# First stage of a two-block transformer kernel: loads interleaved and moved to another queue, the S5 scan split in two halves, top-k searches spaced

## The chip, the cores and the metric

The kernel runs on one core of a Trainium2 chip. The metric is the device time in microseconds (us) of one launch. TensorE is written PE (its weight loads PEld), VectorE DVE, ScalarE ACT, GpSimd POOL, and SyncE SP; SP does nothing here but issue DMAs.

## The reference

Two layers work on `x` of 256 tokens by 2048 features, all in float32.

```python
# block 1
z = rmsnorm(x) @ w_in                 # 2048 x 5128: q, k, v, o, gates, u
hm = mlstm(silu(conv(q,k)), v, gates) # 4 heads of 256, two chunks of 128 tokens
ys = s5_groups(u, ...)                # 64 groups of 16 channels, 64 complex states each:
                                      #   s[t] = a*s[t-1] + B u[t];  y = C s + D u;  GLU
h = x + concat(hm, ys) @ w_out
q = rmsnorm(h) @ wq                   # peer: 8 heads, two halves of 128 keys each
s1, i1 = top_k(q1 @ keys1, 16); s2, i2 = top_k(q2 @ keys2, 16)
idx, gate = top_k over the 256 sums, 16 of them, softmax
h = h + sum_e gate_e * gelu(h . u_tab[idx_e]) * v_tab[idx_e]   # 16384 experts
# block 2: three kinds of attention, gates, and a SwiGLU with 5632 hidden features
```

## The kernel before, in words

**Matrix products.** `gemm` (L245) goes over column tiles of at most 512. For each it loads the weights in chunks of 128 x 1024 (512 KB, two steps of k) by `raw` (L228) into four rotating buffers from SP's queue, splits each half chunk into a rounded part `wh` on ACT (L241) and a rest `wl` on DVE (L242), and runs three matmuls for each of two token blocks (L268 to L270): 12 matmuls of 128 x 512 a chunk. After each chunk it calls `step`, and after each tile a callback that evicts the accumulators.

**Side work.** Everything else is written as generators in three lists (`add_side`). `step` (L169) advances the first generator of each list to its next `yield`, so the number of yields sets behind how many chunks a piece of side work stands in the program. `drain` runs what is left. The queues of the engines are not in program order: `TileContext(nc, schedule_with_timeline_sim=True)` lays them out by simulated times, and takes later work first where its inputs and buffers are ready.

**First stage** (`phase_a`, L744). `x` is loaded in eight pieces, transposed by PE, and evicted to `xh` and `xl` (`put_T`, L306), with the sums of squares on ACT. Then come three tiles of `w_in` that give u and the gates, and eight that give v, q, k, o for two halves of the heads, with two steps a chunk (64 chunks). S5 runs as side work in list 0: `s5_params`, `s5_taps` for each quarter q of the groups, `s5_put_u` (u goes to DRAM and comes back reordered in eight DMAs of 128 KB, in runs of 128 bytes), `s5_in` for each quarter, which writes `Vt`, `s5_states`, a chain of 31 steps of four GpSimd operations over all groups, then for each quarter `s5_out` and `s5_glu`. `s5_out` loads a 1 MB table `t0` back from DRAM, and `s5_glu` moves its result through DRAM in eight DMAs and one load. All these DMAs are SP's. The mixing product `w_out` starts with the S5 half, so it needs `ys`.

**Expert selection** (`peer`). `peer_scores` (L915) runs four tiles of `wq` with one step a chunk. Each tile adds two `tops` generators, each with four searches (L928 to L932). `peer_choose` has 33 yields for each of two token blocks, and its products with one-hots are L986 (DVE), L988 (POOL) and L991 (DVE). `peer_gates` makes the 256 x 16384 gate matrix, two tokens at a time: one-hots on DVE (L1051, L1052), their products with the gates on POOL (L1053, L1054), a matmul (L1060), a copy on ACT (L1063), and sums and products into `AT` on DVE (L1070, L1071, L1073). It yields once, then twice in every fourth of 128 iterations and once in the others: 161 yields. `peer_u` (L1015) runs 32 tiles of 8 chunks with one step a chunk, evicts (L1023, then L1030 or L1034 into `AT`), and calls `drain`. A gate iteration that stands in the program behind the callbacks of n tiles multiplies into what these n tiles have written of `AT`. `peer_v` reads, for each of its products, all 256 tokens of `AT`.

Of the kernel before, what the change touches and what calls it, by code (L numbers as in the profile page):

```python
# [23 lines left out]
D = 2048  # L24
# [95 lines left out]

def later(f):
    yield from f()
# [28 lines left out]
class Kern:  # L151
    def __init__(self, tc, A, ctx):
        self.tc, self.nc, self.A, self.ctx = tc, tc.nc, A, ctx
        self.side = [[], [], []]
        self.GB, self.heads = {}, set()
        self.raw_slots, self.raw_n = [None], 0
# [87 lines left out]

    def gemm(self, wname, widths, KT, xh, xl, cb, steps=1, base=0, ks=None):  # L245

        nc, w = self.nc, self.A[wname]
        off = base
        ka, kb = ks or (0, KT)
        sc = self.stp[1]  # L250
        for i, wn in enumerate(widths):
            P = [self.psG.tile([128, 512], F32, name="g") for _ in range(2)]
            per = RC // wn
            sub = max(1, sc // wn)
            for k0 in range(ka, kb, per):
                kn = min(per, kb - k0)
                r = self.raw(bass.AP(tensor=w.tensor, offset=w.offset + off + 128 * k0 * wn,
                                     ap=[[kn * wn, 128], [1, kn * wn]]), kn * wn)
# [12 lines left out]
                self.step(steps)  # L271
            cb(i, P)
            off += 128 * KT * wn
        return off

    def rstd(self, pool, ss, n, name="rstd", bufs=2):
# [3 lines left out]
        return self.rsqrt(pool, v, name, bufs)  # L280

    def rsqrt(self, pool, v, name, bufs):

        V = self.nc.vector
        w = list(v.shape)
        r = pool.tile(w, F32, name=name, bufs=bufs)
# [30 lines left out]
    def norm_r(self, work, ss, name="rstd"):  # L317
# [3 lines left out]
        return self.rstd(work, st, D, name)  # L321
# [27 lines left out]
    def s5_params(self, p):  # L349
        nc = self.nc  # L350
        prm = p.tile([128, 96 + 2048], F32, name="s5prm")
        nc.sync.dma_start(prm, self.A["s5p"])
# [62 lines left out]
        for r in range(2):  # L415
# [22 lines left out]
        self.Vt = self.xx.tile([128, 32, 2, 32], F32, name="X1")  # L438
        yield

    def s5_taps(self, p, q):
# [38 lines left out]
        nc.sync.dma_start(dr.rearrange("p g o -> p (g o)"), self.A["s5d"][:, q * 256:(q + 1) * 256])  # L480
# [3 lines left out]
        nc.sync.dma_start(bass.AP(tensor=k.tensor, offset=k.offset + q * 16 * 3840 + 7 * 256,  # L484
# [3 lines left out]
    def s5_put_u(self, p, uT):  # L488
# [13 lines left out]
    def s5_in(self, p, q):  # L502
# [21 lines left out]
        for a in range(2):  # L524
            m = 8 * q + 4 * a
            V.tensor_copy(self.Vt[:, :, :, m:m + 4].rearrange("p c r g -> p r g c"), bv[:, a])
        yield

    def s5_states(self, p):

        E, Vt = self.nc.gpsimd, self.Vt
        S = self.S = p.tile([128, 32, 2, 32], F32, name="s5b")
        a8r, a8i = self.a8
        E.memset(S[:, 0], 0.0)
        for c in range(31):
            t1 = p.tile([128, 2, 32], F32, name="s5t1", bufs=2)
            t2 = p.tile([128, 2, 32], F32, name="s5t2", bufs=2)
# [7 lines left out]
    def s5_out(self, p, q, yg):  # L545

        nc, V, q5 = self.nc, self.nc.vector, self.s5
        pw, pn, cn, U, S = q5["pw"], q5["pn"], q5["cn"], self.U[q], self.S
        ms = slice(8 * q, 8 * q + 8)
        t0 = p.tile([128, 8, 16, 16], F32, name="s5t0")  # L550
        k = self.Kd
        nc.sync.dma_start(t0.rearrange("p i g o -> p (i g o)"),
                            bass.AP(tensor=k.tensor, offset=k.offset + q * 16 * 3840,
                                    ap=[[256, 8], [3840, 16], [1, 2048]]))
# [13 lines left out]
        for hf in range(2):  # L568
# [7 lines left out]
            for a in range(2):  # L576
                for r in range(2):
                    for gr in range(4):
                        m = a * 4 + gr
                        nc.tensor.matmul(b[gr * 32:gr * 32 + 32, a * 128:(a + 1) * 128], S[pr, :, r, 8 * q + m],  # L580
# [6 lines left out]
        nc.scalar.activation(yg[:, 16 * q:16 * q + 16].rearrange("p g c -> p (g c)"), b, AF.Gelu)  # L587
        yield

    def s5_glu(self, p, q, yg, ys):  # L590

        nc, V = self.nc, self.nc.vector
# [23 lines left out]
    def s5_all(self, p, uT, ys):  # L616
        yield from self.s5_put_u(p, uT)
        self.glu = p.tile([128, 8, 2, 128], F32, name="s5c")
        self.nc.sync.dma_start(self.glu.rearrange("p a b c -> p (a b c)"), self.A["glu"])
# [5 lines left out]
        yg = self.xx.tile([128, 64, 32], F32, name="X1")  # L625
# [118 lines left out]
    def phase_a(self):  # L744
        nc, V, A = self.nc, self.nc.vector, self.A
        with ExitStack() as ex:
            xh = self.act.tile([128, KD, T], F32R, name="xh")
            xl = self.act.tile([128, KD, T], F32R, name="xl")
            with self.tc.tile_pool(name="pa0", bufs=1) as p0:
                nc.gpsimd.dma_start(self.vecs, A["vecs"])  # L750
                ss = p0.tile([128, 2, 4], F32, name="lss")
                X = [p0.tile([128, D], F32, name=f"X{tb}") for tb in range(2)]
                for q in range(4):
                    s = slice(q * 512, (q + 1) * 512)
                    for tb in range(2):
                        nc.sync.dma_start(X[tb][:, s], A["x"][tb * 128:(tb + 1) * 128, s])
                    self.put_T(X, xh, xl, self.vecs[:, 0:16], q)
                    for tb in range(2):
                        self.sumsq(p0, ss[:, tb, q:q + 1], X[tb][:, s])
                r = self.norm_r(self.c, ss, "rA")  # L760
# [6 lines left out]
            nc.sync.dma_start(bg, A["b_gates"])  # L767
# [70 lines left out]
            for tb in range(2):  # L838
                nc.sync.dma_start(X[tb], A["x"][tb * 128:(tb + 1) * 128, :])
# [75 lines left out]
    def peer_scores(self, p, w, xh, xl, r):  # L915
# [8 lines left out]
        def tops(i, tb, sc):  # L924
            for n in range(4):
# [7 lines left out]
                yield  # L933
# [808 lines left out]
```

## Time and profile before

| | us |
|---|---|
| three runs: median (lowest to highest) | 3687.51 (3687.36 to 3690.19) |
| the profiled execution | 3691.2 |
| its span, first to last instruction | 3689.4 |
| PE busy, share of the span | 3576.1, 97% |
| DVE, ACT, POOL busy | 2710.1, 2007.8, 572.4 |

All stretches below are counted from the span's first instruction. A matmul's recorded end is modelled, so a busy PE means that matmuls follow one another without a gap, and the granted clock (1.00 is the full level) says how fast they run.

### The profile page before, as it was taken

To read this page: it belongs to the slowest core of one execution; us is meant where nothing else is said; L and a number is where in the kernel's file an instruction comes from. 1 tells how busy PE (TensorE), PEld (TensorE's weight loads), DVE (VectorE), ACT (ScalarE), POOL (GpSimd) and SP (SyncE) were. 2 spreads that over 40 slices of the span, in tenths; PEclk is the share of its full clock that TensorE was granted. 3 is DMA by queue.
4 is the path that set the end of the run, shared out by engine and by line. 5 is a ranking of instruction groups with operands and counts; after the bars stand their busy time and mean duration, and the time that the engine had idled before them with its cause. 6 is when DMAs were issued, how large, how long until landed. Compare 5 with 4: busy or idle time off the path is not lost. (4 is left out here: it accounts for less than half of the span.)

```text
span 3689.4 us, 52827 instructions
## 1 busy us (share of the span) xinstructions
PE 3576.1 (97%) x17438; PEld 2959.4 (80%) x17438; DVE 2710.1 (73%) x5604; ACT 2007.8 (54%) x3492; POOL 572.4 (16%) x670
## 2 busy tenths in 40 slices
PE   9897999999999999999999899999999999999999
PEld 7676887788887778888888777887888888888889
DVE  8685779779999857777777878877666666666554
ACT  5555655555555555555555565765445555555443
POOL 1060002225555400001000121001111000000000
PEclk9998999999999999999999999999999999999999
DMA  7656555555555567778777564677776577777665
GB/s 206 184 160 154 185 177 160 169 174 179 172 167 164 169 223 257 255 255 296 257 256 238 197 219 156 190 246 267 257 252 219 171 224 229 232 226 218 186 198 162
DMA packets 228514, 766.07 MB, mean 208 GB/s; under 512 B 40528, under 2 KB 44496, under 8 KB 226192
## 3 DMA queue, kind: packets, MB, share of 16 engines
q1 hardware_dynamic: 197728, 647.89, 55.6%
q0 software_dynamic: 30512, 114.81, 10.2%
q8 instruction: 137, 2.24, 0.2%
q14 instruction: 137, 1.12, 0.1%
HBM read 753.23 MB, written 9.37 MB: 207 GB/s over the span
## 5 line engine op out<-in xcount | busy, mean ns | idle before, releaser
L241 ACT ACTIVATE wh<-raw 128x512 fp32r<-128x512 f32 (+1 forms) x2064 | 1287.5, 628 | 1299.0 <-PE g L269 657.3
L242 DVE TENSOR_TENSOR wl<-raw,wh 128x512 fp32r<-128x512 f32 (+1 forms) x2064 | 1447.1, 715 | 621.7 <-ACT wh L241 534.9
L268 PE MATMUL g<-wh,xl 128*128 128x512 f32 (+2 forms) x3296 | 1269.2, 386 | 12.1 <-ACT wh L241 10.4
L269 PE MATMUL g<-wh,xh 128*128 128x512 f32 (+2 forms) x3296 | 1264.3, 384 | 0.0
L270 PE MATMUL g<-wl,xh 128*128 128x512 f32 (+2 forms) x3296 | 1088.6, 387 | 37.0 <-DVE wl L242 37.0
L270 PEld LDWEIGHTS g<-wl,xh 128*128 128x128 f32 x3296 | 609.5, 189 | 167.1 <-DVE wl L242 58.5
L268 PEld LDWEIGHTS g<-wh,xl 128*128 128x128 f32 x3296 | 623.0, 189 | 133.2 <-ACT wh L241 13.8
L269 PEld LDWEIGHTS g<-wh,xh 128*128 128x128 f32 x3296 | 623.1, 189 | 116.0 <-issue 0.4
L242 DVE TENSOR_TENSOR wl<-xh,wh 128x512 fp32r<-128x512 f32 x206 | 145.2, 706 | 113.7 <-PE g L1110 62.8
L908 POOL DMA_DIRECT2D adac<-in_w_ada x112 | 59.8, 534 | 1049.4 <-DVE adac L904 922.8
L1108 PE MATMUL g<-wh,uev 128*128 128x512 f32 x512 | 200.4, 391 | 6.0 <-ACT wh L241 6.0
L1109 PE MATMUL g<-wh,uev 128*128 128x512 f32 x512 | 200.1, 391 | 0.0
L1108 PE MATMUL b<-wh,uev 128*128 128x512 f32 x512 | 199.4, 390 | 0.0
L1109 PE MATMUL b<-wh,uev 128*128 128x512 f32 x512 | 199.4, 389 | 0.0
L1053 POOL TENSOR_TENSOR e<-e,t 128x256 fp32r<-128x256 f32 x128 | 130.6, 1021 | 316.1 <-DVE e L1052 229.6
L904 DVE SCALAR_TENSOR_TENSOR adac<-adac 128x1024 f32<-128x1024 f32 x112 | 140.4, 1253 | 49.7 <-DMA adac<-in_w_ada 49.5
L241 ACT ACTIVATE wh<-xh 128x512 fp32r<-128x512 f32 x206 | 130.1, 632 | 54.7 <-PE g L1109 36.0
L1110 PE MATMUL g<-wl,uev 128*128 128x512 f32 x512 | 158.4, 390 | 0.0
L268 PE MATMUL g<-wh,fl 128*128 128x512 f32 (+1 forms) x440 | 154.4, 351 | 0.0
L269 PE MATMUL g<-wh,fh 128*128 128x512 f32 (+1 forms) x440 | 154.2, 351 | 0.0
L1054 POOL TENSOR_TENSOR e<-e,t 128x256 fp32r<-128x256 f32 x128 | 145.8, 1139 | 9.9
L908 POOL DMA_DIRECT2D xl<-in_w_ada x80 | 42.3, 529 | 616.6 <-DVE xl L904 616.6
(538 smaller groups left out, 4187.1 us busy)
## 6 DMA issues: line engine op xcount, KB each, us to landing
raw<-in_peer_u SPq DMA_DIRECT2D x256, 512.0 KB, 3.7
raw<-in_w_in SPq DMA_DIRECT2D x192, 512.0 KB, 4.4
raw<-in_w_ffn_in SPq DMA_DIRECT2D x176, 512.0 KB, 4.1
raw<-in_peer_v SPq DMA_DIRECT2D x128, 512.0 KB, 5.4
adac<-in_w_ada POOLq DMA_DIRECT2D x112, 512.0 KB, 5.5
xh<-in_peer_v SPq DMA_DIRECT2D x103, 512.0 KB, 4.5
raw<-in_w_ffn_out SPq DMA_DIRECT2D x88, 512.0 KB, 4.2
xl<-in_w_ada POOLq DMA_DIRECT2D x80, 512.0 KB, 6.2
```

Of the source, the lines that this page charges most:

```text
L241: nc.scalar.activation(h[:, :n], r, AF.Copy)
L242: nc.vector.tensor_tensor(l[:, :n], r, h[:, :n].bitcast(F32), op=OP.subtract)
L268: nc.tensor.matmul(o, xl[:, k - ka, t], hs, start=k == ka, stop=False)
L269: nc.tensor.matmul(o, xh[:, k - ka, t], hs, start=False, stop=False)
L270: nc.tensor.matmul(o, xh[:, k - ka, t], ls, start=False, stop=k == kb - 1)
L904: self.tc.keep_in_program_order(nc.vector.scalar_tensor_tensor(r, r, 1.0, cr, op0=OP.mult, op1=OP.mult, accum_out=self.macc[:, 2 * m + hf: ...
L908: nc.gpsimd.dma_start(r, w[n * 128:(n + 1) * 128, cs])
L1053: E.tensor_tensor(o2[:, :, 1], f(o2[:, :, 0]), bc(f(self.wl), t), op=OP.mult)
L1054: E.tensor_tensor(o2[:, :, 0], f(o2[:, :, 0]), bc(f(self.wh), t), op=OP.mult)
L1108: nc.tensor.matmul(o, w[:, 1, t], h, start=i1 == 0, stop=False)
L1109: nc.tensor.matmul(o, w[:, 0, t], h, start=False, stop=False)
L1110: nc.tensor.matmul(o, w[:, 0, t], l, start=False, stop=i1 == 127)
```

## The change

The first three chunks of `w_in` are issued between the pieces of `x`, and the later three quarters of the transposes become side work in list 2. The transfers of `s5p`, `s5d`, `Kd`, `glu`, `b_gates`, the results of `s5_out` and the second copy of `x` go from SP's queue to POOL's. The eight loads of u are one to a step and pinned behind what stands before them. `s5_states` takes 16 of 32 columns at a time: the first half runs beside the inputs of quarters 2 and 3, the second beside the outputs of 0 and 1. `t0` is loaded ahead. Each search yields twice. Left out below: the `out` argument of `rstd`, `rsqrt` and `norm_r`, and renamed slices.

```diff
+def both(a, b):
+    todo = [a, b]
+    while todo:
+        for g in list(todo):
+            if next(g, g) is g:
+                todo.remove(g)
+        yield
     def raw(self, src, n):
+        if self.raw_begun:
+            return self.raw_begun.pop(0)
...
     def s5_params(self, p):
-        nc.sync.dma_start(prm, self.A["s5p"])
+        nc.gpsimd.dma_start(prm, self.A["s5p"])
...
-        zr = self.xx.tile([64, 7 * 256], F32, name="X1")
+        zr = self.pb.tile([64, 256], F32, name="t", bufs=3)
         nc.gpsimd.memset(zr, 0.0)
-        nc.sync.dma_start(self.Kd.rearrange("q h s c -> (q h) s c")[:, 0:7, :],
-                            zr.rearrange("p (s c) -> p s c", s=7))
+        nc.gpsimd.dma_start(self.Kd.rearrange("q h s c -> (q h) s c")[:, 0:7, :],
+                            zr[:, None, :].to_broadcast([64, 7, 256]))
...
         for j in range(8):
-            nc.sync.dma_start(U[j * 16:(j + 1) * 16], bass.AP(tensor=ud.tensor, offset=ud.offset + j * 32,
-                                                                ap=[[256, 16], [4096, 64], [1, 32]]))
-            if j % 2:
-                yield
+            self.tc.keep_in_program_order(nc.sync.dma_start(
+                U[j * 16:(j + 1) * 16], bass.AP(tensor=ud.tensor, offset=ud.offset + j * 32,
+                                                ap=[[256, 16], [4096, 64], [1, 32]])))
+            yield
...
-    def s5_states(self, p):
+    def s5_states(self, p, h):
-        E, Vt = self.nc.gpsimd, self.Vt
+        E, Vt, ms = self.nc.gpsimd, self.Vt[:, h], slice(16 * h, 16 * h + 16)
...
-            t1 = p.tile([128, 2, 32], F32, name="s5t1", bufs=2)
+            t1 = p.tile([128, 2, 16], F32, name="s5t1", bufs=2)
...
+    def s5_load(self, p, q):
+        self.t0 = p.tile([128, 8, 16, 16], F32, name="s5t0")
+        k = self.Kd
+        self.nc.sync.dma_start(self.t0.rearrange("p i g o -> p (i g o)"),
+                               bass.AP(tensor=k.tensor, offset=k.offset + q * 16 * 3840,
+                                       ap=[[256, 8], [3840, 16], [1, 2048]]))
...
             nc.scalar.activation(YS[:, hf * 256:(hf + 1) * 256], b[:, :256], AF.Copy)
+        if q < 3:
+            self.s5_load(p, q + 1)
...
+    def s5_move(self, q, yg):
...
         for i in range(8):
-            nc.sync.dma_start(bass.AP(tensor=yd.tensor, offset=yd.offset + q * 65536 + i * 32,
-                                      ap=[[256, 16], [4096, 16], [1, 32]]),
-                              yg[i * 16:(i + 1) * 16, 16 * q:16 * q + 16])
+            nc.gpsimd.dma_start(bass.AP(tensor=yd.tensor, offset=yd.offset + q * 65536 + i * 32,
+                                        ap=[[256, 16], [4096, 16], [1, 32]]), yg[i * 16:(i + 1) * 16])
-        nc.sync.dma_start(yT, yd[2 * q:2 * q + 2].rearrange("n p x -> p n x"))
-        for _ in range(6):
-            yield
+        nc.gpsimd.dma_start(yT, yd[2 * q:2 * q + 2].rearrange("n p x -> p n x"))
...
     def s5_all(self, p, uT, ys):
...
-        for q in range(4):
-            if q < 3:
-                yield from self.s5_taps(p, q + 1)
-            yield from self.s5_in(p, q)
-        yield from self.s5_states(p)
-        for q in range(4):
-            yield from self.s5_out(p, q, yg)
-            if q:
-                yield from self.s5_glu(p, q - 1, yg, ys)
-        yield from self.s5_glu(p, 3, yg, ys)
+        def into(qs):
+            for q in qs:
+                if q < 3:
+                    yield from self.s5_taps(p, q + 1)
+                yield from self.s5_in(p, q)
+        def out(qs):
+            for q in qs:
+                yg = yield from self.s5_out(p, q)
+                if q:
+                    yield from self.s5_glu(q - 1, self.yT, ys)
+                self.yT = self.s5_move(q, yg)
+        yield from into((0, 1))
+        yield from both(self.s5_states(p, 0), into((2, 3)))
+        self.s5_load(p, 0)
+        yield from both(self.s5_states(p, 1), out((0, 1)))
+        yield from out((2, 3))
+        for _ in range(6):
+            yield
+        yield from self.s5_glu(3, self.yT, ys)
...
     def phase_a(self):
...
+            for q in range(4):
+                s = slice(q * 512, (q + 1) * 512)
+                for tb in range(2):
+                    nc.sync.dma_start(X[tb][:, s], A["x"][tb * 128:(tb + 1) * 128, s])
+                if q < 3:
+                    first.append(self.raw(self.chunk(A["w_in"], 0, per * q, per, W_IN_TILES[0]), RC))
+            self.raw_begun = first
+            def front():
+                for q in range(1, 4):
+                    self.put_T(X, xh, xl, self.vecs[:, 0:16], q)
+                    if q < 3:
+                        for _ in range(2):
+                            yield
...
+            self.put_T(X, xh, xl, self.vecs[:, 0:16], 0)
...
+            self.add_side(front(), 2)
...
-                nc.sync.dma_start(X[tb], A["x"][tb * 128:(tb + 1) * 128, :])
+                nc.gpsimd.dma_start(X[tb], A["x"][tb * 128:(tb + 1) * 128, :])
...
         def tops(i, tb, sc):
...
                 V.max_index(ix[:, 8:16], v[:, 8:16], c2)
-                yield
+                for _ in range(2):
+                    yield
```

## Rows read from the trace of the kernel before

**Rows 1.** The page's first part: busy us, share of the span, instructions.
```profile
PE 3576.1 (97%) x17438; PEld 2959.4 (80%) x17438; DVE 2710.1 (73%) x5604; ACT 2007.8 (54%) x3492; POOL 572.4 (16%) x670
```

**Rows 2.** Windows: stretch, its length, busy us by engine, granted clock, DMA share, GB/s.
```profile
0.00:20.00 20.00, 12.99 (x51) 10.28 (x52) 12.67 (x30) 15.30 (x38) 7.12 (x15) 1.00 0.89 319
...
93.50:102.00 8.50, 0.03 (x1) 0.03 (x1) 0.05 (x1) 0.71 (x2) 0.00 (x0) 0.81 1.09 293
...
204.00:280.00 76.00, 73.48 (x414) 59.45 (x412) 66.44 (x158) 44.67 (x89) 60.28 (x123) 1.00 0.50 159
280.00:320.00 40.00, 32.07 (x288) 25.20 (x289) 19.78 (x29) 15.09 (x26) 0.00 (x0) 0.87 0.78 159
320.00:352.00 32.00, 22.31 (x157) 16.69 (x156) 20.65 (x43) 22.51 (x35) 0.00 (x0) 0.73 0.51 151
...
480.00:580.00 100.00, 100.00 (x492) 84.12 (x491) 82.36 (x370) 55.43 (x90) 0.00 (x0) 1.00 0.54 167
580.00:680.00 100.00, 88.33 (x373) 67.20 (x372) 96.62 (x222) 45.58 (x71) 37.88 (x16) 0.98 0.49 152
...
1337.00:1352.00 15.00, 8.47 (x29) 6.28 (x28) 6.63 (x9) 8.26 (x12) 1.65 (x3) 0.66 0.88 332
```

**Rows 3.** Waits of PE from 279 to 352: us in total, times, longest.
```profile
PE b L574 <- DMA s5t<-Kd: 7.1, 2, 4.9
PE b L608 <- DMA e<-yd: 5.0, 3, 2.1
```

**Rows 4.** Timeline of SP's queue from 73 to 104: start, us of issue, count.
```profile
77.28 0.77 SPq L232 DMA_DIRECT2D raw<-in_w_in  x1
79.66 11.98 SPq L495 DMA_DIRECT2D X<-ud  x8
91.68 1.51 SPq L619 DMA_DIRECT2D s5c<-in_glu  x1
93.69 9.91 SPq L232 DMA_DIRECT2D raw<-in_w_in  x5
```

**Rows 5.** S5 chain by line: duration ns least/median/most, first and last start, shape.
```profile
L526 DVE COPY X<-b x8: 605/621/634, 120.9 to 203.1; 128x256 f32<-128x256 f32 x8
...
L540 POOL TENSOR_TENSOR s5t<-s5t,X x31: 312/367/1302, 203.8 to 267.9; 128x64 f32<-128x64 f32 x31
...
L848 DVE TENSOR_TENSOR s5b<-ys,s5t x4: 684/692/692, 328.3 to 345.6; 128x512 fp32r<-128x512 f32 x4
```

**Rows 6.** GpSimd's groups from 200 to 272: busy us and mean ns, idle before.
```profile
L540 POOL TENSOR_TENSOR s5t<-s5t,X 128x64 f32<-128x64 f32 x31 | 17.4, 563 | 51.3 <-DVE X L526 51.3
```

**Rows 7.** DMA issues: KB each and us to landing; one POOL issue by line.
```profile
yd<-X SPq DMA_DIRECT2D x32, 32.0 KB, 4.4
...
L908 POOL DMA_DIRECT2D adac<-in_w_ada x112: 527/527/699, 2073.7 to 3376.0; - x112
```

**Rows 8.** Selection by line: duration ns least/median/most, first and last start, shape.
```profile
L988 POOL TENSOR_TENSOR AT<-AT x16: 1735/2146/4782, 590.0 to 671.9; 128x800 f32<-128x800 f32 x16
...
L1060 PE MATMUL b<-e,O x256: 274/278/388, 782.5 to 1276.4; 128*128 128x256 f32 x128
...
L1023 ACT ACTIVATE uev<-g,rB x64: 670/678/692, 572.7 to 1338.7; 128x512 f32<-128x512 f32 x64
```

**Rows 9.** Timeline of ACT: eviction of the ninth tile of `peer_u`.
```profile
770.67 1.25 ACT L1023 ACTIVATE uev<-g,rB 128x512 f32<-128x512 f32 x2
```

**Rows 10.** Gate iterations from 1200 to 1278, by line: busy us and mean ns.
```profile
L1071 DVE TENSOR_TENSOR AT<-AT,macc 128x128 f32<-128x128 f32 (+3 forms) x38 | 10.8, 313 | 0.0
L1052 DVE TENSOR_TENSOR e<-iota,t 128x256 fp32r<-128x256 f32 x19 | 8.7, 458 | 0.0
...
L1070 DVE TENSOR_TENSOR macc<-b,macc 128x128 f32<-128x128 f32 (+3 forms) x38 | 8.3, 258 | 0.1
L1051 DVE TENSOR_TENSOR O<-iota,t 128x256 fp32r<-128x256 f32 x19 | 7.9, 416 | 2.9 <-PE b L1060 2.9
...
L1054 POOL TENSOR_TENSOR e<-e,t 128x256 fp32r<-128x256 f32 x19 | 24.0, 1264 | 1.5
L1053 POOL TENSOR_TENSOR e<-e,t 128x256 fp32r<-128x256 f32 x19 | 21.5, 1133 | 30.1 <-DVE e L1052 21.7 <-PE g L269 4.5 <-PE b L1060 3.5
```

More of the change, by code (lines that the diff above doesn't have):

```diff
@@ L243, in split, with chunk @@
         return h, l
+    def chunk(self, w, off, k0, kn, wn):
+        return bass.AP(tensor=w.tensor, offset=w.offset + off + 128 * k0 * wn, ap=[[kn * wn, 128], [1, kn * wn]])
     def gemm(self, wname, widths, KT, xh, xl, cb, steps=1, base=0, ks=None):
@@ L256, in gemm @@
                 kn = min(per, kb - k0)
-                r = self.raw(bass.AP(tensor=w.tensor, offset=w.offset + off + 128 * k0 * wn,
-                                     ap=[[kn * wn, 128], [1, kn * wn]]), kn * wn)
+                r = self.raw(self.chunk(w, off, k0, kn, wn), kn * wn)
                 for j0 in range(0, kn, sub):
@@ L274, in gemm, with rstd, rsqrt @@
         return off
-    def rstd(self, pool, ss, n, name="rstd", bufs=2):
+    def rstd(self, pool, ss, n, name="rstd", bufs=2, out=None):
         v = pool.tile(list(ss.shape), F32, name=name + "v", bufs=bufs)
         self.nc.vector.tensor_scalar(v, ss, 1.0 / n, EPS, op0=OP.mult, op1=OP.add)
-        return self.rsqrt(pool, v, name, bufs)
-    def rsqrt(self, pool, v, name, bufs):
+        return self.rsqrt(pool, v, name, bufs, out)
+    def rsqrt(self, pool, v, name, bufs, out=None):
         V = self.nc.vector
         w = list(v.shape)
-        r = pool.tile(w, F32, name=name, bufs=bufs)
+        r = pool.tile(w, F32, name=name, bufs=bufs) if out is None else out
         t = pool.tile(w, F32, name=name + "t", bufs=bufs)
@@ L315, in put_T, with norm_r @@
                 V.scalar_tensor_tensor(xl[:, k], pi, g, xh[:, k].bitcast(F32), op0=OP.mult, op1=OP.subtract)
-    def norm_r(self, work, ss, name="rstd"):
+    def norm_r(self, work, ss, name="rstd", out=None):
         st = work.tile([128, 2], F32, name="nst")
         self.nc.vector.tensor_reduce(st, ss, axis=AX.X, op=OP.add)
-        return self.rstd(work, st, D, name)
+        return self.rstd(work, st, D, name, out=out)
     def norm_T(self, X, r, xh, xl, work, gain, shift, row=None):
@@ L433, in s5_params @@
         self.Kd = self.dram.tile([4, 16, 15, 256], F32, name="Kd")
[L434 removed]
+        zr = self.pb.tile([64, 256], F32, name="t", bufs=3)
         nc.gpsimd.memset(zr, 0.0)
[L436 to L438 removed]
+        nc.gpsimd.dma_start(self.Kd.rearrange("q h s c -> (q h) s c")[:, 0:7, :],
+                            zr[:, None, :].to_broadcast([64, 7, 256]))
+        self.Vt = self.xx.tile([128, 2, 32, 2, 16], F32, name="X1")
         yield
@@ L479, in s5_taps @@
         dr = self.pb.tile([128, 16, 16], F32, name="t", bufs=3)
-        nc.sync.dma_start(dr.rearrange("p g o -> p (g o)"), self.A["s5d"][:, q * 256:(q + 1) * 256])
+        nc.gpsimd.dma_start(dr.rearrange("p g o -> p (g o)"), self.A["s5d"][:, q * 256:(q + 1) * 256])
         nc.gpsimd.tensor_tensor(dr, dr, self.ident[:, None, :16].to_broadcast([128, 16, 16]), op=OP.mult)
@@ L524, in s5_in @@
         for a in range(2):
-            m = 8 * q + 4 * a
-            V.tensor_copy(self.Vt[:, :, :, m:m + 4].rearrange("p c r g -> p r g c"), bv[:, a])
+            m = 8 * (q % 2) + 4 * a
+            V.tensor_copy(self.Vt[:, q // 2, :, :, m:m + 4].rearrange("p c r g -> p r g c"), bv[:, a])
         yield
-    def s5_states(self, p):
-        E, Vt = self.nc.gpsimd, self.Vt
-        S = self.S = p.tile([128, 32, 2, 32], F32, name="s5b")
-        a8r, a8i = self.a8
+    def s5_states(self, p, h):
+        E, Vt, ms = self.nc.gpsimd, self.Vt[:, h], slice(16 * h, 16 * h + 16)
+        S = self.S[:, h]
+        a8r, a8i = (z[:, :, ms] for z in self.a8)
         E.memset(S[:, 0], 0.0)
         for c in range(31):
-            t1 = p.tile([128, 2, 32], F32, name="s5t1", bufs=2)
-            t2 = p.tile([128, 2, 32], F32, name="s5t2", bufs=2)
+            t1 = p.tile([128, 2, 16], F32, name="s5t1", bufs=2)
+            t2 = p.tile([128, 2, 16], F32, name="s5t2", bufs=2)
             E.tensor_tensor(t1, a8r, S[:, c], op=OP.mult)
@@ L579, in s5_out @@
                         m = a * 4 + gr
-                        nc.tensor.matmul(b[gr * 32:gr * 32 + 32, a * 128:(a + 1) * 128], S[pr, :, r, 8 * q + m],
+                        nc.tensor.matmul(b[gr * 32:gr * 32 + 32, a * 128:(a + 1) * 128], S[pr, :, r, 8 * (q % 2) + m],
                                          G2[pr, r, m].rearrange("p i o -> p (i o)"),
@@ L584, in s5_out @@
             nc.scalar.activation(YS[:, hf * 256:(hf + 1) * 256], b[:, :256], AF.Copy)
+        if q < 3:
+            self.s5_load(p, q + 1)
         yield
         b = self.transpose4([YS[:, i * 128:(i + 1) * 128] for i in range(4)])
-        nc.scalar.activation(yg[:, 16 * q:16 * q + 16].rearrange("p g c -> p (g c)"), b, AF.Gelu)
+        yg = self.xx.tile([128, 16, 32], F32, name="ssj")
+        nc.scalar.activation(yg.rearrange("p g c -> p (g c)"), b, AF.Gelu)
         yield
-    def s5_glu(self, p, q, yg, ys):
-        nc, V = self.nc, self.nc.vector
+        return yg
+    def s5_move(self, q, yg):
+        nc = self.nc
         if q == 0:
@@ L618, in s5_all @@
         self.glu = p.tile([128, 8, 2, 128], F32, name="s5c")
[L619 to L630 removed]
+        self.nc.gpsimd.dma_start(self.glu.rearrange("p a b c -> p (a b c)"), self.A["glu"])
+        self.S = p.tile([128, 2, 32, 2, 16], F32, name="s5b")
+        def into(qs):
[17 more added lines that the diff above has]
+        yield from self.s5_glu(3, self.yT, ys)
     def mlstm_gates(self, p, gt):
@@ L748, in phase_a @@
             xl = self.act.tile([128, KD, T], F32R, name="xl")
[L749 to L752, printed above, removed]
+            first = []
+            nc.gpsimd.dma_start(self.vecs, A["vecs"])
+            X = [self.xx.tile([128, D], F32, name=f"X{tb}") for tb in range(2)]
+            per = RC // W_IN_TILES[0]
+            for q in range(4):
[5 more added lines that the diff above has]
+            self.raw_begun = first
+            r = self.c.tile([128, 2], F32, name="rA", bufs=2)
+            def front():
[4 more added lines that the diff above has]
+                            yield
+                ss = mp.tile([128, 2, 4], F32, name="lss")
                 for q in range(4):
-                    s = slice(q * 512, (q + 1) * 512)
                     for tb in range(2):
[L756 to L760, printed above, removed]
+                        self.sumsq(self.xx, ss[:, tb, q:q + 1], X[tb][:, q * 512:(q + 1) * 512])
+                    if q == 1:
+                        yield
+                self.norm_r(self.c, ss, "rA", r)
+            self.put_T(X, xh, xl, self.vecs[:, 0:16], 0)
             s5 = ex.enter_context(self.tc.tile_pool(name="s5", bufs=1))
```

20 lines of the change are left out of this document (10 added, 10 removed).

## The prediction

> **What bounds the kernel now.** I read the page's busy times first, then windows over the stages that the change touches, then PE's waits, SP's queue and the S5 chain, and last the place of the expert gates. PE is busy for 97% of the span [rows 1], so only time in which PE idles, or runs below full clock, can be won.
>
> The windows show where that is [rows 2]. From 93.5 to 102 PE does nothing: 8.5 us. From 280 to 320 it lacks 7.9 us, and the granted clock of 0.87 costs 0.13 x 40 = 5.2 us more; from 320 to 352 it lacks 9.7 us, and 0.73 costs 0.27 x 32 = 8.6. Together 39.9 us, which is all that the first stage can give back. From 480 to 580, while the searches run, PE is busy for 100.0 of 100 us: they cost nothing now. From 580 to 680 it lacks 11.7 us and DVE is busy for 96.6.
>
> The first gap has its cause in SP's queue: eight loads of u keep it for 11.98 us and the `glu` table for 1.51, and between the weight chunk of 77.28 and the next of 93.69 no weights are issued [rows 4]. The loss from 280 on is the end of the S5 chain: PE waits for the `t0` tables (7.1 us) and for the results that come back through DRAM (5.0) [rows 3]. That chain is a ladder: the last copies into `Vt` at 203.1, the scan from 203.8 to 267.9, the last piece of the `w_out` input at 345.6 [rows 5]. From the scan's end to there, four quarters take 345.6 + 0.7 - 268.6 = 77.7 us, 19.4 each.
>
> **The change part by part.**
>
> *Start.* PE is busy for 13.0 of the first 20 us [rows 2]. The interleaved load lets the product begin sooner, but the 24 moved transposes, their evictions and the sums of squares are still to be done, now beside the splits, and 319 GB/s flow there already. It can win at most the 7.0 us of idle time, and lose as much if early side loads take the place of weights. I take -1 (-4 to +2).
>
> *Loads of u.* Eight issues of 1.5 us now stand among four weight chunks of 0.4 to 0.8 us: 12 + 2 = 14 us of SP time, which four chunks already buffered can cover. The gap of 8.5 us should close (0 to 8.5). I count it only as far as it moves the S5 chain: the second quarter's input, a third of the way from 120.9 to 203.1 [rows 5], so at 148.3, comes some 3 us earlier, at 145.
>
> *The scan in halves.* The operations double, to 2 x 31 x 4, at half the width. A step of four takes (268.6 - 203.8) / 31 = 2.09 us now [rows 5]. No row has the half shape. If the price went with the width, a half would take 32 us; if width did not matter, 65. The group's mean is 563 ns [rows 6] where the least is 312 [rows 5]: nearly half of it is no work of its own, and DVE is busy for 66.4 of 76 us beside it [rows 2]. So I stand near the upper end: 57 us a half, 114 for both. Between them POOL issues two results of nine DMAs, at 0.53 us [rows 7] 9.5 us, and each last one waits for eight writes, 4.4 us to landing [rows 7]: 18 us (0 to 25). The second scan ends at 145 + 114 + 18 = 277 (209 to 300).
>
> The Trainium skill (SBUF — State Buffer, section "Who interferes with whom") says that a DVE instruction with two SBUF inputs and a GpSimd instruction that reads SBUF hold the shared port in turn, each for its whole length. The row agrees so far, from 312 to 1302 ns for one shape; by that rule a half-width operation waits as long as a full one, and the sum would use 65 us a half.
>
> *Outputs.* Behind the second scan only two quarters are left: 2 x 19.4 = 39 us, so the S5 half of the `w_out` input is ready at 316 (no earlier than 306, where PE's own work would end: 346 less 39.9; 339 at the late end) instead of 346.3. That is -30 (-40 to -7). The prefetched `t0` may take some of the 7.1 us more. The first two quarters run under weight chunks; POOL's queue is late there only for the scan, which I have counted.
>
> *Other moved transfers.* `s5p`, `s5d`, `Kd`, the gate bias and the second x leave SP: a few issues of 0.5 us, behind weights already buffered. 0 (-2 to +2).
>
> *Searches at half pace.* This moves more than the searches. Steps after the first `wq` tile: 24, then 256 in `peer_u`, 280. Yields now: 8 x 4 = 32 of the searches, 66 of the choice, 161 of the gates, 259: 21 to spare. After: 64 + 66 + 161 = 291, which is 11 too many. The gates do keep their place: they should start in the tenth tile, and their first matmul at 782.5 [rows 8] follows the ninth tile's eviction at 770.67 [rows 9]; they should end at chunk 235, which at (1338.7 - 572.7) / 31 = 24.7 us a tile is 1274, and the last is at 1276.4 [rows 8]. The choice does not keep its place (it should end at chunk 74, near 777; its products end at 672 [rows 8]), since nothing ties it to a tile. A gate iteration is tied to the evictions before it.
>
> So 11 yields, which are eight of the 128 iterations, fall into the `drain` behind the last tile, and `peer_v` cannot start before them, as it reads all tokens of `AT`. An iteration costs DVE 416 + 458 + 2 x 258 + 2 x 313 = 2.02 us and POOL 1133 + 1264 = 2.40 [rows 10]; eight are 16.2 to 19.2 us, with no weights to multiply. I take +18 (12 if two run ahead, 23 with one pass through the chain on top). Where PE idles there now, from 1337 to 1352, the clock is already 0.66 [rows 2]; I add nothing for it. On the other side I credit nothing: 480 to 580 has no loss, and the loss of 580 to 680 is the choice's, whose place is not set by yields.
>
> **Sum.** -1 - 30 + 0 + 18 = -13. On the profiled 3691.2 (its span 3689.4) that is 3678.2. The profiled run is 3.7 above the median of 3687.51, so I say 3674.
>
> **The rivals.** Changes within 0.2%, 7.4 us, are about what a measurement here cannot tell from none.
>
> A, as forecast: -13, own range -24 to -3, 3664 to 3685. Chance 0.48.
>
> B, GpSimd becomes the bound. For: doubled operations, the port shared with a busy DVE, 36 DMAs in the same queue, and waits on DRAM in front of scan steps. At 65 us a half and 25 for transfers the second scan ends at 300, S5 at 339, and PE waits there for it: -7 - 1 + 18 = +10, 3697. It decides as soon as the second scan ends after 290: then the gates' 18 us are no longer paid for. Against: steps beside a quieter DVE cost less than the mean, and S5's inputs may come sooner. By the skill's rule above, this is the case. Chance 0.21.
>
> C, the drained gates cost nothing: the layout by simulated times finds room, or iterations run before the last evictions. For: the choice ran 105 us ahead of its place. Against: rows 8 and 9 show the gates at theirs. -31, 3656. Chance 0.14.
>
> D, weights still starve. The loads of u need the DMA engines whatever their order, and POOL's transfers now compete with the weights; PE, in order, may also wait mid-stage for a table. About 8.5 us remain: -13 + 8.5 = -4.5, 3683. For: a DMA share of 1.09 in the gap [rows 2]. Against: 204 to 280 has a share of 0.50. Chance 0.17. The Trainium skill (DMA: Bandwidth & Descriptors, "Issuing engines are not separate DMA queues") holds that issuing from several engines saves issue time only; by that rule moving `glu` wins its 1.51 us of issue and none of its transfer.
>
> **The numbers.** A holds the prediction, 3674. From 3653 (C's centre and a little more) to 3694 (short of B's centre) leaves out less than half of B and of C, and the ends of the rest: some 2 in 10. Faster by over 7.4 us: 0.40 of A, 0.14 of C, 0.06 of D: 0.60. Slower: 0.12 of B and 0.01 of D, 0.13. The rest, 0.27, is the same.
>
> **What would show it.** The gap at 93 gone, and weights between the loads of u. Twice 31 steps on POOL, the second half ending near 277; the last `w_out` input near 316, `w_out` following without a long gap. No change from 480 to 680. The gates' first matmul some 95 us later within `peer_u`, and eight iterations behind its last eviction, with PE nearly empty for about 18 us more. Wrong would be a scan ending after 290 (B), no matmul of the gates behind the last eviction (C), or a gap of PE near 90 to 105 (D).

## The result, and the profile after

The changed kernel takes 3735.93 us in the median (3734.2 to 3747.84), the kernel before 3688.85 on the same chip: ratio 1.0127 (1.0115 to 1.014), 47 us slower. The prediction was 3674, with a range from 3653 to 3694. The profiled execution's span is 3732.8, 43.4 more than before.

Five points of the two traces say where the 43.4 us arise. They are starts of single instructions: the last S5 piece of the `w_out` input (L900, before L848), the first and the last eviction of `peer_u` (L1076, L1023), and the first matmul of `peer_v` (L1161, L1108); then the span's end. First and last starts, changed (two lines) and before:
```profile
L900 DVE TENSOR_TENSOR s5b<-ys,s5t x4: 680/690/692, 329.6 to 355.3; 128x512 fp32r<-128x512 f32 x4
L1076 ACT ACTIVATE uev<-g,rB x64: 671/679/692, 589.0 to 1356.4; 128x512 f32<-128x512 f32 x64
```
```profile
L1108 PE MATMUL g<-wh,uev x512: 389/389/792, 1346.1 to 2039.0; 128*128 128x512 f32 x171
```

| | last S5 input | first `peer_u` eviction | last one | first `peer_v` matmul | end |
|---|---|---|---|---|---|
| before | 345.6 | 572.7 | 1338.7 | 1346.1 | 3689.4 |
| changed | 355.3 | 589.0 | 1356.4 | 1386.9 | 3732.8 |
| later by | 9.7 | 16.3 | 17.7 | 40.8 | 43.4 |

So 16 us are lost ahead of `peer_u`, where 31 were to be won in the first stage, and 23 between the last `peer_u` tile and `peer_v`, where 18 were to be lost.

The windows of the changed kernel (columns as in [rows 2]; 400 to 420 and 1357 to 1387 are new):
```profile
80.00:105.00 25.00, 19.78 (x145) 15.36 (x144) 10.79 (x26) 11.10 (x23) 1.28 (x2) 0.86 0.98 248
204.00:280.00 76.00, 69.39 (x474) 55.34 (x472) 61.34 (x152) 41.82 (x83) 67.99 (x156) 0.98 0.56 173
280.00:320.00 40.00, 25.03 (x184) 19.91 (x184) 15.82 (x33) 13.25 (x22) 6.05 (x11) 0.82 0.53 124
320.00:352.00 32.00, 20.20 (x157) 15.55 (x158) 8.10 (x13) 13.76 (x23) 10.95 (x19) 0.77 0.47 142
400.00:420.00 20.00, 12.45 (x54) 9.67 (x53) 15.51 (x86) 10.82 (x34) 0.00 (x0) 0.83 0.14 48
480.00:580.00 100.00, 100.00 (x490) 84.14 (x489) 74.14 (x286) 53.95 (x90) 0.00 (x0) 1.00 0.54 173
580.00:680.00 100.00, 90.34 (x395) 69.83 (x393) 96.62 (x297) 50.19 (x77) 33.23 (x14) 1.00 0.49 154
1357.00:1387.00 30.00, 6.75 (x23) 4.38 (x21) 22.54 (x62) 9.06 (x18) 12.51 (x19) 0.55 0.47 173
```
Against [rows 2], PE lacks 15 us instead of 7.9 from 280 to 320, and it has a new hole of 7.5 us near 400 (0.9 before), where DMA hardly moves anything (share 0.14) and PE's one long wait is for a head, not for weights. From 480 to 580 nothing changed, as forecast. From 1357 to 1387 PE is nearly empty. From 80 to 105 it lacks 5.2 us; before:
```profile
80.00:105.00 25.00, 16.52 (x133) 13.32 (x132) 7.12 (x22) 9.90 (x22) 0.75 (x1) 0.87 1.21 205
```

PE's waits from 279 to 420, the answer to [rows 3]:
```profile
PE b L632 <- DMA e<-yd: 28.6, 3, 13.0
PE b L313 <- DVE ml_rm L750: 5.1, 1, 5.1
```
The `t0` wait of 7.1 us is gone, as hoped, but PE waits 28.6 us instead of 5.0 for S5's results on their way back from DRAM. The reason stands in GpSimd's queue, behind the last scan step:
```profile
272.28 0.25 POOL L555 TENSOR_TENSOR s5b<-s5t,s5t 128x32 f32<-128x32 f32 x1
272.82 0.62 POOL L891 DMA_DIRECT2D X<-in_x  x1 [0.29 <-issue]
273.44 3.93 POOL L619 DMA_DIRECT2D yd<-ssj  x7
278.54 0.56 POOL L619 DMA_DIRECT2D yd<-ssj  x1 [1.18 <-DMA X<-in_x]
287.79 0.75 POOL L622 DMA_DIRECT2D e<-yd  x1 [8.69 <-DMA yd<-ssj]
...
300.44 4.46 POOL L619 DMA_DIRECT2D yd<-ssj  x8 [11.78 <-ACT ssj L608]
316.81 0.73 POOL L622 DMA_DIRECT2D e<-yd  x1 [11.91 <-DMA yd<-ssj]
321.39 4.46 POOL L619 DMA_DIRECT2D yd<-ssj  x8 [3.85 <-ACT ssj L608]
...
339.11 4.48 POOL L619 DMA_DIRECT2D yd<-ssj  x8 [8.98 <-ACT ssj L608]
```
The scan ends at 272.5, better than the 277 forecast. But all four moves (L619 writes, L622 reads back) come behind it. The first quarter's Gelu ran at 252.1, and its first write goes out at 273.44; the second quarter's Gelu itself comes behind the scan:
```profile
252.10 0.60 ACT L608 ACTIVATE ssj<-b 128x512 f32<-128x512 f32 x1
...
299.55 0.60 ACT L608 ACTIVATE ssj<-b 128x512 f32<-128x512 f32 x1
```

The gates (L1113) around the last eviction at 1356.4, on PE, then on DVE, then one line of ACT:
```profile
1356.00 0.42 PE L1113 MATMUL b<-e,O 128*128 128x256 f32 x2
1356.52 1.23 PE L313 MATMUL b<-ident,uev 128*128 128x128 f32 x8
1358.46 0.51 PE L1113 MATMUL b<-e,O 128*128 128x256 f32 x2 [0.71 <-POOL e L1107]
1362.83 1.37 PE L1113 MATMUL b<-e,O 128*128 128x256 f32 x4 [3.87 <-POOL e L1107]
1371.79 0.80 PE L1113 MATMUL b<-e,O 128*128 128x256 f32 x2 [7.59 <-POOL e L1107]
...
1380.45 0.80 PE L1113 MATMUL b<-e,O 128*128 128x256 f32 x2 [1.40 <-ACT macc L1116]
1386.85 0.80 PE L1161 MATMUL g<-wh,uev 128*128 128x512 f32 x1 [5.60 <-DVE uev L1149]
```
```profile
1363.23 0.48 DVE L1124 TENSOR_TENSOR AT<-AT,macc 128x128 f32<-128x128 f32 x2
1368.55 0.69 DVE L254 TENSOR_TENSOR wl<-xh,wh 128x512 fp32r<-128x512 f32 x1 [4.84 <-ACT wh L253]
1369.16 0.42 DVE L1104 TENSOR_TENSOR O<-iota,t 128x256 fp32r<-128x256 f32 x1
```
```profile
1366.94 1.06 ACT L953 ACTIVATE xl<-xl 128x1024 f32<-128x1024 f32 x1 [3.40 <-DMA xl<-in_c]
```
From 1358 on there are 16 products: eight iterations, two matmuls each. In their midst DVE stands idle for 4.84 us: the split of a `peer_v` weight is queued ahead of the next iteration's one-hots, and its rounded part on ACT (L253) stands behind L953, which waits 3.40 us for a load of the input `c`, issued at 1357.18.

### The profile page after: what moved, and what is told of

It reads as the page before. It is cut to its first block, busy times and chain, and to the rows that moved or that the text cites. A ratio compares the mean times of both kernels' runs of the same rounds, so it can differ in the third digit from the quotient of the medians.

```text
span 3732.8 us, 52989 instructions
## 1 busy us (share of the span) xinstructions
PE 3581.2 (96%) x17438; PEld 2964.2 (79%) x17438; DVE 2708.0 (73%) x5615; ACT 1997.4 (54%) x3496; POOL 634.2 (17%) x845
## 4 chain that ended last, share of the span: by engine, by line
PE 81%; issue 7%; POOL 5%; DVE 4%; DMA 3%; ACT 0%; SPq 0%; DVEq 0%; POOLq 0%; ACTq 0%
PE g L284 20%; PE g L282 19%; PE g L283 19%; PE g L1161 3%; PE g L1162 3%; PE g L1163 3%; PE b L1161 3%; PE b L1162 3%; PE b L1163 3%; PE b L313 2%; DVE wl L254 2%; POOL s5b L555 1%; PE b L1113 1%; POOL s5t L552 1%; POOL s5t L554 1%
## 5 line engine op out<-in xcount | busy, mean ns | idle before, releaser
L253 ACT ACTIVATE wh<-raw 128x512 fp32r<-128x512 f32 (+1 forms) x2064 | 1286.4, 628 | 1347.9 <-PE g L283 640.9
L1161 PE MATMUL g<-wh,uev 128*128 128x512 f32 x512 | 200.3, 391 | 5.6 <-DVE uev L1149 5.6
L1161 PE MATMUL b<-wh,uev 128*128 128x512 f32 x512 | 199.6, 390 | 1.1 <-ACT wh L253 1.1
L1106 POOL TENSOR_TENSOR e<-e,t 128x256 fp32r<-128x256 f32 x128 | 126.5, 988 | 414.9 <-DVE e L1105 251.5
L254 DVE TENSOR_TENSOR wl<-xh,wh 128x512 fp32r<-128x512 f32 x206 | 133.6, 687 | 68.5 <-ACT wh L253 66.5
L1163 PE MATMUL b<-wl,uev 128*128 128x512 f32 x512 | 157.7, 389 | 0.0
L253 ACT ACTIVATE wh<-xh 128x512 fp32r<-128x512 f32 x206 | 130.0, 632 | 50.1 <-PE g L1162 47.5
L1107 POOL TENSOR_TENSOR e<-e,t 128x256 fp32r<-128x256 f32 x128 | 138.3, 1081 | 9.7
```

The source lines that it names most:

```text
L253: nc.scalar.activation(h[:, :n], r, AF.Copy)
L254: nc.vector.tensor_tensor(l[:, :n], r, h[:, :n].bitcast(F32), op=OP.subtract)
L1106: E.tensor_tensor(o2[:, :, 1], f(o2[:, :, 0]), bc(f(self.wl), t), op=OP.mult)
L1107: E.tensor_tensor(o2[:, :, 0], f(o2[:, :, 0]), bc(f(self.wh), t), op=OP.mult)
L1161: nc.tensor.matmul(o, w[:, 1, t], h, start=i1 == 0, stop=False)
L1163: nc.tensor.matmul(o, w[:, 0, t], l, start=False, stop=i1 == 127)
```

## The experiments

Ratios are to the kernel before, timed beside it, with their 95% interval in brackets; the us given with them are the difference of two ratios times 3690.

**The moves' queue.** Writes and read back on SP:
```
-            nc.gpsimd.dma_start(bass.AP(tensor=yd.tensor, ...
+            nc.sync.dma_start(bass.AP(tensor=yd.tensor, ...
-        nc.gpsimd.dma_start(yT, yd...
+        nc.sync.dma_start(yT, yd...
```


> The changed kernel with the moves of S5's results (eight writes and one read back for each quarter) on SP's queue, as before the change; all else as changed. Queue theory: the first quarter's result is ready at 252 us but its writes are issued at 273.4, because they stand behind the whole second scan in GpSimd's queue; the other quarters hang one behind the other on it. Without that queue the first move goes out near 253, the first glu products run before 275, the last S5 input of w_out comes near 336 instead of 355, and the time falls by 15 to 25 us. Ladder theory (PE's order and the pacing set the quarters, the queue does not matter): the second quarter still comes out near 298 and the time falls by under 8 us.

1.0089 (1.0075 to 1.0104), 14 us less than the changed kernel. SP's queue:
```profile
255.03 9.62 SPq L619 DMA_DIRECT2D yd<-ssj  x8
...
266.26 0.38 SPq L622 DMA_DIRECT2D e<-yd  x1
```
The first move is out at 255 instead of 273; PE's wait for read backs falls from 28.6 to 4.2 us, and the last S5 input from 355.3 to 341.3. The queue theory gave the size a little high. The second quarter's Gelu, at 287.2, still comes behind the scan's end at 276.4.

Moves on GpSimd, but each scan step's first operation kept behind what was traced ahead of it:
```
-            E.tensor_tensor(t1, a8r, S[:, c], op=OP.mult)
+            self.tc.keep_in_program_order(E.tensor_tensor(t1, a8r, S[:, c], op=OP.mult))
```


> The changed kernel with the moves left on GpSimd's queue, but each scan step kept in the program's order there, so that the first quarter's move stands in the middle of the second scan and the second quarter's at its end. Queue theory: the first move goes out near 255; the scan waits some 10 to 15 us for it and ends near 287; two quarters are left behind it, the last S5 input of w_out comes near 335 to 345, and the time falls by 8 to 20 us. Ladder theory: the delayed scan costs its 10 to 15 us and nothing is won, so the time stays or grows by up to 10 us.

1.0105 (1.009 to 1.012): 8 us less, though the intervals of the two kernels overlap a little. The first writes start at 258.17, the read back at 269.84; the scan's last step slips to 312.7, further than I expected, and still the last S5 input comes at 347.8, 7.5 us sooner. So a better place in the same engine's queue wins about half of what the other queue wins.

**The gates.** One yield in place of two:
```
-                for _ in range(2):
-                    yield
+                yield
```


> The changed kernel with one yield for each search, as before the change. Overflow theory: the eight gate iterations no longer fall behind the last peer_u tile; their first product comes about 95 us earlier, none stands behind the last eviction, and the time falls by 23 us (19 to 27). Rival (the searches at half pace win something themselves while wq runs): the fall is smaller by what PE then loses between 480 and 700 us, down to nothing.

1.0071 (1.0058 to 1.0084): 21 us less. Products of the gates run from 801.9 to 1295.9, none behind the last eviction at 1358.2, and `peer_v` starts 7.9 us behind that instead of 30.5 (7.4 before).

> The kernel before with the second yield for each search and nothing else of the change. Overflow theory: the same eight iterations fall behind the last tile, and the time grows by 23 us (18 to 27), to about 3711. Rival (the overflow costs only together with the changed first stage, or the searches win something): it grows by under 10 us.

1.0056 (1.0043 to 1.0069): 21 us more than before. 16 products behind the last eviction, 28.6 us to `peer_v`. The same cost without the new first stage.

Searches left at half pace, the gates' double yield thinned:
```
-            for _ in range(2 if t0 % 8 == 0 else 1):
+            for _ in range(2 if t0 % 16 == 0 else 1):
```


> The changed kernel with the double yield of the gates at every sixteenth token instead of every eighth: 145 yields instead of 161, 275 in all for 280 steps, with the searches left at half pace. Overflow theory: nothing falls behind the last tile, and the time falls by the same 21 us as with one yield for each search (17 to 25). Rival (the searches' pace itself costs): it falls by less than 8 us.

1.0081 (1.0067 to 1.0094): 17 us less, no product behind the last eviction. So it is the count of yields, not the searches' pace.

**The parts together, and the second x.** On SP:
```
-                nc.gpsimd.dma_start(X[tb], A["x"][tb * 128:(tb + 1) * 128, :])
+                nc.sync.dma_start(X[tb], A["x"][tb * 128:(tb + 1) * 128, :])
```


> The changed kernel with three parts undone together: S5's moves on SP, the second load of x on SP, one yield for each search. If the two costs measured singly (14 us for the moves, 21 for the gates) add up, it is 35 us under the changed kernel, 12 us over the kernel before (8 to 16). What is left is then the 13 us in which PE waits near 400 us for the second half's mLSTM heads. If they share a cause, the time stays 20 us or more over the kernel before.

1.0102 (1.0085 to 1.0118), 25 us above what I expected. PE's longest wait and SP's queue show why:
```profile
PE g L282 <- ACT wh L253: 26.4, 1, 26.4
```
```profile
226.72 16.36 SPq L244 DMA_DIRECT2D raw<-in_w_in  x7
271.60 0.33 SPq L891 DMA_DIRECT2D X<-in_x  x1
272.02 0.60 SPq L563 DMA_DIRECT2D s5t<-Kd  x1
272.72 1.09 SPq L244 DMA_DIRECT2D raw<-in_w_in  x2
```
The load of x goes into the buffer that the scan reads (its last step there starts at 271.7), so it waits for the scan's end; SP issues nothing from 243.1 to 271.6, and weights wait behind it. Without this edit:

> The changed kernel with two parts undone: S5's moves on SP and one yield for each search; the second x stays on GpSimd's queue. With the three parts undone PE waited 26.4 us for one weight split, while the load of x stood at 271.6 in SP's queue in front of weights. If that load alone was what kept the time up, the two parts add: 35 us under the changed kernel, 12 us over the kernel before (8 to 16). If the moves on SP's queue hold up weights themselves once the gates are back, it stays 20 us or more over.

1.0023 (1.0014 to 1.0032): 8.5 us over before. The two costs add up, and the move of x to GpSimd's queue is worth keeping beside the divided scan.

**The order of the last tiles.** Empty yields ahead of the third quarter and of the last glu, first (with x on SP) 12 and 30, then (x on GpSimd) 12 and 21:
```
+        for _ in range(12):
+            yield
         yield from out((2, 3))
-        for _ in range(6):
+        for _ in range(30):
```


> The kernel of the three parts undone, with empty yields put in (12 ahead of the third quarter, 30 instead of 6 ahead of the last glu), so that the tiles of q and k of the second half stand ahead of the last S5 quarter in the program, as they do before the change. Order theory: their evictions no longer wait in PE's and ACT's queues behind the last quarter's read back; the heads start near 360 instead of 372, the wait of 13 us near 400 is gone, and the time is 9 to 15 us under that of the three parts undone, about the kernel before or a little under. Pacing theory (the heads are late because w_out comes sooner): the wait stays, at most 4 us are won.

1.0139 (1.0123 to 1.0156), 14 us more than with x on SP alone, where I expected less. The last glu now stands behind the heads: the last S5 input comes at 405.8, and `w_out` stands still from 366 until then. PE's waits within the heads are not gone either: 10.9 us up to 377, then 4.2 and 3.2. The next expectation says otherwise of the wait near 400; the trace does not bear that out.

> The same two parts undone, with empty yields (12 ahead of the third quarter, 21 instead of 6 ahead of the last glu), so that the program's order is that of before the change: both tiles, then the last glu, then the second half's heads. With 30 yields the wait near 400 us was gone, but the last glu stood behind the heads and came 37 us later. Order theory: here the wait of 13 us is gone and the last S5 input comes no later than 350 us; the time is 6 to 15 us under that of the two parts undone, within 6 us of the kernel before. Rival (what the one gives the other takes: heads and glu share PE's and ACT's queues): within 4 us of the two parts undone.

1.0001 (0.9992 to 1.001): 8 us less than with the two parts undone, and the kernel before again. The heads' first matmul (L725, here L727) falls from 376.5 to 360.8, and PE's 5.1 us of waiting for a head are gone. PE's longest wait from 345 to 480 without the empty yields, then its two longest with them:
```profile
PE b L313 <- DVE ml_sm L737: 5.1, 1, 5.1
```
```profile
PE g L282 <- DVE s5b L902: 4.1, 1, 4.1
PE g L282 <- DVE s5q L916: 1.0, 1, 1.0
```

**The division taken away.** One scan of 31 full steps behind all inputs, with the functions of before for it; the start, the pinned loads of u and the moved side loads as changed.

> The changed first stage without the division: one scan of 31 full steps behind all inputs, outputs behind it, moves and second x on SP, one yield for each search, all as before; the new start, the spread loads of u, and the moved side loads stay as changed. Division theory: no wait near 400 us, and what the start and the loads of u win (5 to 7 us by chunk 100 in the trace of the changed kernel) is kept in part: 0 to 8 us under the kernel before. Rival (the moved loads and the new start set the later loss): 8 us or more over it.

1.0048 (1.0035 to 1.0061): 18 us over, as the rival had it, but not for its reason. The next run undoes only the pin and the four extra yields:
```
-            self.tc.keep_in_program_order(nc.sync.dma_start(...))
-            yield
+            nc.sync.dma_start(...)
+            if j % 2:
+                yield
```


> The undivided first stage again, now with the loads of u as before the change (unpinned, four yields for eight loads); the new start and the moved side loads stay. Yield theory: the four extra yields put the whole S5 chain back by some 5 to 10 us (the scan began at 214.5 instead of 203.9), so the scan begins near 206 and the time is 10 to 18 us under that of the undivided stage, within 6 us of the kernel before. Rival (the new start or the loads moved to GpSimd's queue set it): less than 5 us are won.

1.001 (1.0001 to 1.002): 14 us less. The copies into `Vt`, here without and then with the old loads of u:
```profile
L540 DVE COPY X<-b x8: 609/621/633, 129.2 to 212.9; 128x256 f32<-128x256 f32 x8
```
```profile
L540 DVE COPY X<-b x8: 605/620/636, 119.9 to 202.3; 128x256 f32<-128x256 f32 x8
```
Four more yields put the whole chain back by 9 to 11 us. It is not the pin: the eight loads stand together on SP's queue in both, from 82.6 and from 81.6.

**The loads of u by themselves**, in the kernel before, on GpSimd's queue:
```
-            nc.sync.dma_start(U[j * 16:(j + 1) * 16], ...
+            nc.gpsimd.dma_start(U[j * 16:(j + 1) * 16], ...
```


> The kernel before with the eight loads of u issued on GpSimd's queue, in the same yields, and nothing else. Queue theory: SP's 12 us of issue are free, weights go on, PE's wait of 8.5 us near 95 closes, and the time falls by 4 to 9 us. Transfer theory (the small packets of u keep the DMA engines themselves busy, whoever issues them): the wait stays above 5 us and the time moves by less than 3 us.

1.0007 (0.9998 to 1.0017). PE's waits for weight splits from 80 to 204, before and with this edit:
```profile
PE g L268 <- ACT wh L241: 9.6, 2, 8.5
```
```profile
PE g L268 <- ACT wh L241: 4.2, 2, 3.2
```
The longest falls from 8.5 to 3.2 us, and `peer_u` starts 3.9 us sooner; the time does not show it. So 5.3 us of the gap went with SP's queue; 3.2 stay with the loads on GpSimd's.

**Was the gain there to be had?**
```
-        E.memset(S[:, 0], 0.0)
-        for c in range(31):
+        E.memset(S, 0.0)
+        for c in range(8):
```


> The kernel before with 8 of the 31 scan steps; it leaves out the other 23 (the states behind are zero), with their yields, so that the whole S5 chain comes some 30 us sooner for nothing: an ideal case of what the division of the scan was forecast to win. Forecast theory: w_out's S5 half is ready near 315 and the time falls by 25 to 31 us. Second-wall theory: the second half's mLSTM heads end near 398 in the kernel before, just where the S5 half of w_out is used up; a sooner S5 lets PE run into them, it waits there for 10 to 25 us, and the time falls by less than 12 us.

0.9995 (0.9985 to 1.0006): nothing, and neither theory saw why. The first Gelu runs 33 us sooner, but the last S5 input only 4.4 (341.2). SP's queue:
```profile
246.56 3.83 SPq L597 DMA_DIRECT2D yd<-X  x8
250.48 27.36 SPq L232 DMA_DIRECT2D raw<-in_w_in  x11
277.90 0.43 SPq L601 DMA_DIRECT2D e<-yd  x1
```
The read back stands behind eleven weight chunks, and the second Gelu is at 288.3, against 296.8 before.

Two output stages in each round beside the second scan, on top of the spaced kernel:
```
-        yield from both(self.s5_states(p, 1), out((0, 1)))
+        yield from both(self.s5_states(p, 1), pairs(out((0, 1))))
```


> The spaced kernel with S5's moves on SP and one yield for each search, and two output stages instead of one in each round beside the second scan, so that the second quarter should be out before the scan's end, and only two quarters are left behind it. If the second quarter's place is what was missing: its Gelu falls from 286 to near 265, the last S5 input from 345 to near 325, and the time falls by 10 to 20 us against the spaced kernel. Second-wall theory: S5 may come sooner but the heads do not, and the time stays within 5 us of the spaced kernel.

0.9998 (0.9989 to 1.0007). Now the second Gelu is at 264.0, ahead of the scan's end, and the last S5 input at 334.1, 11 us sooner than before the change. Of that, 6.4 are left at the first `peer_u` eviction (566.3) and nothing at `peer_v` (1346.4). The lead goes within `peer_u`, between the evictions at 1082 (7.4 us ahead) and 1270 (0.3). PE's wait for the gates' products on GpSimd from 950 to 1400 and the window in question, before and then here:
```profile
PE b L1060 <- POOL e L1054: 10.5, 10, 2.2
1100.00:1250.00 150.00, 141.10 (x671) 115.99 (x670) 138.72 (x372) 76.39 (x143) 86.25 (x75) 1.00 0.53 164
```
```profile
PE b L1123 <- POOL e L1117: 12.3, 9, 2.2
1100.00:1250.00 150.00, 140.50 (x649) 115.03 (x648) 132.53 (x355) 72.74 (x136) 83.23 (x73) 0.97 0.52 157
```
The waits differ by 1.8 us only; the granted clock of 0.97 instead of 1.00 costs some 0.03 x 150 = 4.5 us. Why it was lower here was not tried.

## Why the prediction was wrong

The step that failed is the one on the outputs: "Behind the second scan only two quarters are left", and with it "POOL's queue is late there only for the scan, which I have counted". All four were left. I had counted the moves in GpSimd's queue as a delay of the scan (18 us between the halves), and not asked the reverse, how long a move waits for the scan. The layout put all scan steps first, so the first quarter's result, ready at 252, left at 273. From the scan's end to the last S5 input the four quarters then took 355.3 + 0.7 - 272.5 = 83.5 us, 20.9 each, close to the 19.4 of the prediction. The term of -30 came out as +16 at the first `peer_u` eviction.

The queue is 14 us of this, by the run with the moves on SP. It does not explain all that was missing: there the second quarter still came behind the scan, since `both` takes one of its stages for each scan yield. With two stages in a round, only two quarters were left, but they took 334.1 + 0.7 - 278.1 = 56.7 us instead of 39, in part for the empty yields, and what was won did not reach `peer_v`. The term also took for granted that an S5 input sooner than before shortens the kernel. No run shows it: 4.4 us sooner (the cut scan) and 11 us sooner (two stages in a round) left the time at 0.9995 and 0.9998.

A second part of that +16 was in no term: what is late next. S5's last quarter stood ahead of the evictions of the second half's q and k tiles in PE's and ACT's queues, since the six empty yields ahead of three of the glus were gone and two paired stages take one yield; so the mLSTM heads began at 385.3 instead of 357.9, and `w_out` ran out of S5 work near 400. The spaced kernel shows its worth: 8 us.

**The other steps.** Start: forecast -1; the 51st weight split ends at 78.3 instead of 78.9: right. Loads of u: the gap did not close, PE wins 3.3 us from 80 to 105; the eight loads still stand together on SP, and the chain came 4 to 5 us later (copies into `Vt` from 124.9 to 208.1) instead of 3 sooner, because I did not count their four extra yields. The scan: forecast 57 us a half; the first runs from 158.5 to 215.2, the second from there to 272.5: right, 57 each. That its end came near the forecast 277 is partly luck: it began at 157.4 instead of 145, and the 18 us of moves did not arise, as they came behind it. Other moved transfers: right at about nothing (the undivided stage with the old loads of u is 4 us over the kernel before), but only as the second x stayed off SP, as the 26.4 us show.

On the price of a half: the four lines of a step took 514 ns in the mean before (62.7 us for 122 operations from 203 to 269; the 563 of [rows 6] are one line of the four) and 446 after (109.7 for 246 from 155 to 275). Their least went from some 315 to some 250, so what an operation took beyond its least stayed at 196 to 199 ns, and 124 x 65 ns = 8 us are all that the half width won: 65 - 8 = 57. The rule on the shared port (Trainium skill, SBUF — State Buffer, "Who interferes with whom") speaks of the wait alone, and the trace agrees, as far as two stretches can be compared; the 65 that I drew from it left out the operation's own, shorter time.

Searches: the mechanism was right to the iteration, eight behind the last eviction. The size was +18 and is 23 in the trace, 21 by the runs; the stall of DVE behind an early `peer_v` split, 4.84 us, was not in it.

**The rivals.** B had the sign and named GpSimd's queue, but as a delay of the scan: it was to decide if the second scan ended after 290, and it ended at 272.5. C is refuted by the 16 products. D's gap remained in part, but is not what made the time. The rule beside D (Trainium skill, DMA: Bandwidth & Descriptors, "Issuing engines are not separate DMA queues") fits the gap of u: another issuer won 5.3 of 8.5 us, not all.

**What stays open.** With the queue, the gates and the order mended, the time is the kernel before's, so these three account for the loss. Why the last S5 input came only 4.4 us sooner with 23 scan steps left out, whether by the read back's place or by the stages' pace, was not separated. And from the first `peer_v` matmul to the end, where the code is the same in all, the profiles take 2342 to 2352 us (2343.3 before, 2345.9 changed); a gain of 3 us is lost in that, and its cause was not tried.

## What to carry to other kernels

A transfer moved to another engine's queue can stand behind that engine's work, as the moves did here for 21 us, or hold up what is behind it, as the load of x did: before moving one, write down what is ahead of it in the new queue at the moment its data is ready, and what will be behind it. Where work is paced by yields, a yield added or dropped anywhere shifts all that is traced later; count steps against yields for the whole stage. And for a gain at the end of one chain, look up when the next input of the same consumer is ready: here the heads ended at 398, just as the S5 half of `w_out` was used up.

## What the runs showed of the hardware

In a quiet stretch a scan operation of half the width takes 250 ns, against 312 at full width [rows 5]: much of its time does not go with the width. On GpSimd's queue the read back waited 8.69 us for the last of eight writes at a DMA share of 0.44, 11.91 at 0.93, and 2.48 at 0.28 in the last quarter.
